# ScalarE takes copies, one table set for the residual norms, and softmax sums turned on TensorE

## The chip, the cores and the metric

The kernel runs on one core of a Trainium2 chip. The core has TensorE (PE, matrix products into PSUM), VectorE (DVE), ScalarE (ACT), GpSimd (POOL) and SyncE (SP), which here issues the DMAs. The engines run side by side and wait for each other through semaphores; each engine and each DMA-issuing queue works its own instructions in program order. The metric is the device time of one execution in microseconds (us), from the first instruction to the last, all data in float32. Every product of two matrices is made of three matmuls: both factors are split into a high and a low part, and high by high, low by high and high by low are summed (lines L165 to L167).

## The reference

A network of four layers on a sequence of 1024 tokens with 1024 features: a gated linear attention (GLA), a dilated sliding-window attention (SWA), a differential attention (DA) and a latent attention (MLA). Behind each stands a residual with a norm. The parts that the change touches:

```python
def layer_norm(x, g, b):                      # behind GLA and SWA
    mu = jnp.mean(x32, axis=-1, keepdims=True)
    xc = x32 - mu
    var = jnp.mean(xc * xc, axis=-1, keepdims=True)
    return (xc * lax.rsqrt(var + LN_EPS) * g + b)
...
def _rmsnorm(x, g):                           # ahead of DA and MLA, in both, and at the end
    return x * lax.rsqrt(jnp.mean(x * x, axis=-1, keepdims=True) + RMS_EPS_2) * g
...
def block(qb):                                # DA, 128 queries by 1024 keys, 8 heads
    sc = jnp.einsum('bqhcd,bkhcd->bhcqk', qb, k) * scale
    p = jax.nn.softmax(sc, axis=-1)
    p = p[:, :, 0] - lam * p[:, :, 1]
    return jnp.einsum('bhqk,bkhd->bqhd', p, v)
...
o = _rmsnorm(o, subln_g) * (1.0 - lambda_init)
o = o * jax.nn.silu(z)
return o @ w_out
...
q = _rmsnorm(q_a, q_a_norm_g) @ w_q_b         # MLA's low-rank products
kv = _rmsnorm(c_kv, kv_a_norm_g) @ w_kv_b
```

## The kernel before

All activations lie transposed, features on the 128 partitions and tokens along the row, so a norm's sum over features is a product with a matrix of ones on PE. The program runs GLA (to about 395 us of the span), a boundary (to 545), SWA (to 1215), a boundary (to 1346), DA (V products and modulation to 1460, its main loop to 1991, a drain to 2018), a boundary (to 2148), MLA (low-rank products to 2290, the rest to 2690) and the last boundary, which ends the program.

**A boundary** (`boundary`) takes the attention output `o` and the gate `z` from DRAM for each of 8 feature tiles and 2 halves of the tokens: `gated` computes Silu(z)*o, 16 calls in all, the result split into `oh` and `ol`. It multiplies by the output weights, adds the residual, squares (L706, sums in `acc`), sums on PE (`stat`, L717), and makes 1/sqrt as Exp(-0.5*Ln(mean+eps)) on ACT: `rstd`, L722 and L723. A layer norm ahead of a modulated norm calls `rstd` twice per half. Then come the scaled tiles `t` (L773, L774) and their halves `xh` (L775) and `xl`, on which the next stage's first products wait. Silu, Ln and Exp need tables on ACT; where the next function isn't in the set at hand, an ACT_TABLE_LOAD stands ahead of it, put there by the build.

**Fill** work is queued as units of small pieces (a product's feature tiles) in `Fill`, and given out between the steps of a stage by a budget. `u_t` makes 128x512 products, `u_v` 128x256 ones, both in PSUM tiles `mm` that turn over, so a tile that isn't copied out holds up a later product. The copies out: `u_gate` (L254, z to DRAM; half 0 on ACT, half 1 on DVE), SWA's V (L959) and DA's V (L1285, both alternately DVE and ACT), MLA's low-rank results `lraw` (L1485, DVE, followed by Square on ACT, L1487). `lownorm` norms these (L1506 Ln, L1507 Exp, L1510 scaling on DVE). `u_ada` computes modulation columns: DVE multiplies rows of a streamed weight by a scalar and adds up (`xb`, L575 to L577), PE sums the partitions with ones (L583).

**DA's main loop** has 64 iterations, 8 heads of 8 query blocks. Each makes scores of two softmaxes (`sc`, L1420), a maximum on DVE (L1424), Exp on ACT with the sum of a row in `d0` (`dsum`) and `den` (L1426), and one iteration later their combination on DVE (L1441 to L1443). Two iterations later P is transposed on PE (`attend`, L1240) and split on ACT and DVE into `PTh` and `PTl` (`PTl` at L150), and after each second block `pv` multiplies by V (L1365 to L1368) and writes `y` to DRAM as `d_o`. The norm of DA's output is put off: `norm` writes sums of squares to DRAM (`d_ms`), `combine` writes the softmax sums (`d_dn`, L1445), and `factors` reads both back as `vr` (L1251, L1252) in another layout, computes an inverse square root by four Newton steps on DVE (L1254 to L1265) and writes `d_rs`, which the boundary reads. It is called after the norm of head 6 for 14 half heads (tiles 128x56), once for (7,0) (128x4) and in the boundary for (7,1).

**The order** of PE in DA's loop is written out as in the code; the other engines and SP's queue are set by a scheduler that simulates the program. A DMA that has to wait holds all behind it on SP.

## Time and profile before

| what | us |
|---|---|
| median of 3 runs | 2798.11 (2795.3 to 2800.18) |
| the profiled execution's own time | 2794.63 |
| its span | 2792.9 |
| PE busy in it | 2660.9 (95%) |
| DVE busy | 1890.0 (68%) |
| ACT busy | 1349.2 (48%) |

The profile is of one execution. An engine's busy time is the sum of its instructions; a waiting engine shows idle time ahead of an instruction, with the engine, line and operation that released it. The granted clock of TensorE is given as a share of full speed, 2.4 GHz; half of it is 1.2 GHz. Times inside the profile are microseconds from the start of the span.

### The profile page before, as it was taken

The page shows a single profiled execution, that of the slowest core. Times are in us where ns is not written, and L with a number is a line of the kernel's source. Part 1 is how long each engine was busy: PE and PEld are TensorE (multiplying, and loading weights), DVE is VectorE, ACT ScalarE, POOL GpSimd, SP SyncE. Part 2 cuts the span into 40 slices and gives each one's busy share as a digit, 9 for nine tenths or more (in the row PEclk, how much of TensorE's full clock was granted, in tenths as well). Part 3 has the DMA queues.
Part 4 walks back from the last instruction along what each step waited for, and adds up shares of the span by engine and source line. Part 5 has one row for each costly group of instructions (what it writes and reads, how often), then busy time and mean ns, then how long its engine had stood idle before and what let it go on. Part 6 is the DMA issues. An engine that isn't in the chain of part 4 may idle for free.

```text
span 2792.9 us, 39308 instructions
## 1 busy us (share of the span) xinstructions
PE 2660.9 (95%) x14788; PEld 2234.5 (80%) x14788; DVE 1890.0 (68%) x3478; ACT 1349.2 (48%) x2492; POOL 314.6 (11%) x224
## 2 busy tenths in 40 slices
PE   8999999998999999988999999998799899999998
PEld 7889988887778878776897877786578688888878
DVE  7776547567666666667657788886576627777785
ACT  5444345426344434347515766765445415554563
POOL 0000000000000000000015656664000000000000
PEclk9999999999999999999999999999799999999999
DMA  5310155654111111154642432342275220100143
GB/s 206 107 43 32 49 180 182 210 176 144 50 42 50 46 47 53 50 185 145 228 165 74 63 67 61 66 55 62 90 266 170 68 70 23 33 27 29 39 172 110
DMA packets 163926, 274.70 MB, mean 98 GB/s; under 512 B 32948, under 2 KB 82388, under 8 KB 162072
## 3 DMA queue, kind: packets, MB, share of 16 engines
q1 hardware_dynamic: 163736, 272.19, 31.7%
q8 instruction: 116, 1.90, 0.3%
q14 instruction: 74, 0.61, 0.1%
HBM read 195.48 MB, written 66.17 MB: 94 GB/s over the span
## 4 chain that ended last, share of the span: by engine, by line
PE 67%; DVE 14%; DMA 7%; ACT 7%; issue 3%; SPq 1%; POOL 1%; ACTq 0%; DVEq 0%; POOLq 0%
PE mm L165 14%; PE mm L166 14%; PE mm L167 14%; PE pt L1240 3%; PE sc L1420 3%; PE sc L1657 2%; PE sc L1049 2%; PE lv L489 1%; PE pt L1153 1%; PE sc L166 1%; PE sc L165 1%; PE sc L167 1%; DVE den L1424 1%; PE mm L1623 1%; DVE wlo L150 1%
## 5 line engine op out<-in xcount | busy, mean ns | idle before, releaser
L165 PE MATMUL mm<-xh,whi 128*128 128x512 f32 x1456 | 613.3, 421 | 18.0 <-DVE t L911 6.0
L167 PE MATMUL mm<-xh,wlo 128*128 128x512 f32 x1456 | 574.0, 394 | 2.5 <-POOL wlo L150 1.6
L166 PE MATMUL mm<-xl,whi 128*128 128x512 f32 x1456 | 574.0, 394 | 1.7 <-DVE xl L150 1.7
L165 PEld LDWEIGHTS mm<-xh,whi 128*128 128x128 f32 x1456 | 277.6, 191 | 75.5 <-DVE t L911 7.3
L167 PEld LDWEIGHTS mm<-xh,wlo 128*128 128x128 f32 x1456 | 275.8, 189 | 64.4 <-POOL wlo L150 2.5
L166 PEld LDWEIGHTS mm<-xl,whi 128*128 128x128 f32 x1456 | 277.6, 191 | 52.9 <-DVE xl L150 4.0
L150 POOL TENSOR_TENSOR wlo<-wraw,whi 128x1024 fp32r<-128x1024 f32 x29 | 70.6, 2435 | 1334.9 <-ACT whi L192 1332.9
L165 PE MATMUL mm<-wvhi,xh 128*128 128x256 f32 x704 | 204.6, 291 | 4.8 <-DVE V L959 3.0
L192 ACT CAST whi<-wraw 128x1024 fp32r<-128x1024 f32 (+2 forms) x141 | 135.9, 964 | 138.3 <-PE mm L166 128.9
L167 PE MATMUL mm<-wvhi,xl 128*128 128x256 f32 x704 | 199.2, 283 | 0.1
L166 PE MATMUL mm<-wvlo,xh 128*128 128x256 f32 x704 | 198.6, 282 | 0.0
L1426 ACT ACTIVATE P<-sc,den 128x1024 f32<-128x1024 f32 x128 | 142.9, 1117 | 113.4 <-DVE den L1424 112.8
L1424 DVE TENSOR_REDUCE den<-sc 128x1 f32<-128x1024 f32 x128 | 153.5, 1212 | 3.5 <-PE sc L1420 3.5
L150 DVE TENSOR_TENSOR wlo<-wraw,whi 128x1024 fp32r<-128x1024 f32 (+2 forms) x113 | 123.5, 1093 | 43.8 <-ACT whi L192 40.7
L1043 ACT ACTIVATE P<-P,nm 128x128 f32<-128x128 f32 (+1 forms) x192 | 84.9, 443 | 124.5 <-DVE nm L1041 124.2
L165 PEld LDWEIGHTS mm<-wvhi,xh 128*128 128x128 f32 x704 | 134.0, 190 | 9.9 <-DVE V L959 3.2
L166 PEld LDWEIGHTS mm<-wvlo,xh 128*128 128x128 f32 x704 | 134.5, 191 | 1.3 <-issue 1.0
L167 PEld LDWEIGHTS mm<-wvhi,xl 128*128 128x128 f32 x704 | 133.9, 190 | 0.4 <-DVE xl L150 0.4
L165 PE MATMUL mm<-oh,xh 128*128 128x512 f32 (+1 forms) x336 | 126.1, 375 | 0.3 <-ACT oh L796 0.3
L166 PE MATMUL mm<-ol,xh 128*128 128x512 f32 (+1 forms) x336 | 124.2, 370 | 2.0 <-DVE ol L150 2.0
L167 PE MATMUL mm<-oh,xl 128*128 128x512 f32 (+1 forms) x336 | 123.7, 368 | 0.0
L1053 DVE CUSTOM_DVE_ANT_0 P<-sc,band 128x128 f32<-128x128 f32 (+1 forms) x192 | 59.6, 348 | 71.5 <-PE sc L1049 71.1
(355 smaller groups left out, 6124.5 us busy)
## 6 DMA issues: line engine op xcount, KB each, us to landing
xa<-in_ada_w SPq DMA_DIRECT2D x12, 2048.0 KB
d_z<-zt SPq DMA_DIRECT2D x64, 256.0 KB
oh<-d_z SPq DMA_DIRECT2D x64, 256.0 KB
ol<-d_o SPq DMA_DIRECT2D x64, 256.0 KB
d_r<-X SPq DMA_DIRECT2D x48, 256.0 KB
wraw<-in_swa_wq SPq DMA_DIRECT2D x24, 512.0 KB
res<-d_r SPq DMA_DIRECT2D x40, 256.0 KB
zt<-zt SPq DMA_DIRECT2D x160, 64.0 KB
```

Source lines behind the costliest of these rows:

```text
L150: eng.tensor_tensor(out, src, hi.bitcast(F32), op=OP.subtract)
L165: mm(ps, l[0], r[0], start=first, stop=False)
L166: mm(ps, l[0], r[1], start=False, stop=False)
L167: mm(ps, l[1], r[0], start=False, stop=last)
L192: nc.scalar.copy(hi, raw)
L1043: S.activation(p[:, off:off + w_], p[:, off:off + w_], AF.Exp, bias=nm[:, g, b:b + 1], scale=scale, accum_out=stat(h, g, 1, b))
L1049: T.matmul(sc[:, b % 2, :w_], q[:, b * 128:b * 128 + 128], k[:, k0:k0 + w_], start=True, stop=True)
L1053: V.tensor_tensor_reduce(p[:, off:off + w_], sc[:, b % 2, :w_], mk, 1.0, NEG, op0=OP.add, op1=OP.max, accum_out=stat(h, g, 0, b))
L1240: nc.tensor.transpose(pt[:, i, :], P[:, (4 * j + i) * 128:(4 * j + i) * 128 + 128], self.ident)
L1420: T.matmul(sc[c][:, s], QS[h][c][r, q0:q0 + 128], (KL[h] if k else KH[h][c])[r, s], start=first, stop=not first)
L1424: V.tensor_reduce(dn[:, 2 + c:3 + c], sc[c], AX, OP.max, negate=True)
L1426: S.activation(p, sc[c], AF.Exp, bias=dn[:, 2 + c:3 + c], accum_out=dn[:, 1:2] if c else d0)
```

## The change

Six edits, of which the fourth has two places.

1. `tables`: an explicit load of table set 6, which holds Ln and Exp, is put behind the 16th Silu of each boundary. The build's loads at L722, L723, L1506 and L1507 go: 11, 11, 3 and 3 loads; 4 new ones come.
2. Copies out of PSUM on ACT: all of SWA's V (12 move from DVE), all of DA's V (16), MLA's `lraw` (10), and half 1 of the gate in MLA's low-rank part (8).
3. The softmax sums are turned on PE: instead of a DMA that scatters `dsum` (128 partitions by 4 elements) into `d_dn` element by element, `pv` transposes it into an unused part of its PSUM bank, ACT copies the 4x128 result to `dr` and SP writes four rows of 512 bytes. There are 16 of these.
4. `factors` issues its reads where it did, and returns its arithmetic, `rest`, which the loop calls two iterations later. In DA's V products the modulation units `ada` stand further back among the V units; in MLA's low-rank part the last one stands behind two gate units.
5. One tile of ones serves both uses.
6. In GLA, in SWA's loop and in DA's, the gate keeps its engines (`act=False`).

```diff
+    def tables(self, n, behind):
+        nc = self.nc
+        with self.tc.issue_after(behind.ins):
+            return nc.scalar.add_instruction(mybir.InstLoadActFuncSet(
+                act_func_set_id=n, name=nc.get_next_instruction_name(), engine=mybir.EngineType.Activation))
...
-            (self.nc.vector.tensor_copy if hf else self.nc.scalar.copy)(z, ps)
+            (self.nc.scalar.copy if act or not hf else self.nc.vector.tensor_copy)(z, ps)
...
-            S.activation(g, z, AF.Silu)
+            silu = S.activation(g, z, AF.Silu)
+            if len(O) == 15:
+                self.tables(6, silu)
...
-                        (S.copy if st % 2 else V.tensor_copy)(Vt[g][:, st, :], ps)
+                        S.copy(Vt[g][:, st, :], ps)
...
+        def rest():
+            V.scalar_tensor_tensor(e, e, 128.0 * 1e-6, e, op0=OP.mult, op1=OP.mult)
+            V.tensor_tensor(t, t, e, op=OP.add)
...
+        return rest
...
-                    (S.copy if st % 2 else V.tensor_copy)(t, ps)
+                    S.copy(t, ps)
...
-                    pre.add(u_vs(0, range(4, 8)), u_vs(1, range(4, 5)), ada[0], u_vs(1, range(5, 8)), ada[1], u_vs(2, range(0, 4)), ada[2], u_vs(2, range(4, 8)), ada[3], u_vs(3, range(0, 4)), ada[4], u_vs(3, range(4, 8)), ada[5])
+                    pre.add(u_vs(0, range(4, 8)), u_vs(1, range(4, 8)), ada[0], u_vs(2, range(0, 3)), ada[1], u_vs(2, range(3, 6)), ada[2], u_vs(2, range(6, 8)), u_vs(3, range(0, 1)), ada[3], u_vs(3, range(1, 4)), ada[4], u_vs(3, range(4, 8)), ada[5])
...
-                o = self.mmp.tile([128, 256], F32, name="mm")
+                bank = self.mmp.tile([128, 512], F32, name="mm")
+                o, d = bank[:, :256], bank[0:4, 256:384]
...
+                if due:
+                    T.transpose(d, due[0][2], self.ident)
...
+                if due:
+                    g, hf, _ = due.pop()
+                    r = dp.tile([128, 128], F32, name="dr")
+                    S.copy(r[0:4], d)
+                    nc.sync.dma_start(self.dnd[g][:, half(hf)].rearrange("o (f p) -> (o f) p", p=128), r[0:4])
...
-                    self.factors(dp, FACT[h, qb4])
+                    return self.factors(dp, FACT[h, qb4])
...
+                if facts and facts[0][0] <= i:
+                    facts.pop()[1]()
...
-                            nc.sync.dma_start(self.dnd[h][:, half(t // 4)].rearrange("o (f p) -> (o p) f", p=128),
-                                              dsum[:, t - 3:t + 1])
+                            due.append((h, t // 4, dsum[:, t - 3:t + 1]))
...
-                        V.tensor_copy(raw[key, hf][:, c, :], ps)
+                        S.copy(raw[key, hf][:, c, :], ps)
...
-                pre.add(self.u_ada(p0, 1, 5, 1), *[self.u_gate(h, "mla_wz", p0) for h in range(3, 8)])
+                late = [self.u_gate(h, "mla_wz", p0) for h in range(3, 8)]
+                pre.add(*late[:2], self.u_ada(p0, 1, 5, 1), *late[2:])
```

Lines below L254 move down by 6 to 24 in the new file (L722 is L728, L775 is L781, L1251 is L1260, L1254 is L1265, L1255 is L1266, L1485 is L1508). What stands where, at the three places that matter most, first ACT in the boundary to DA, where the norm of the second half is made between the modulated tiles of the first (`t` and the halves `xh_70`), before:

```order
L774 ACTIVATE t<-t,mods,gsc 128x512
L722 ACT_TABLE_LOAD
L722 ACTIVATE rs<-stat,cv 128x512
L775 CAST xh_70<-t 128x512
L204 CAST wvhi<-wvraw 128x512
L723 ACT_TABLE_LOAD
L723 ACTIVATE rs<-rs 128x512
L204 CAST wvhi<-wvraw 128x512
```

and now:

```order
L780 ACTIVATE t<-t,mods,gsc 128x512
L728 ACTIVATE rs<-stat,cv 128x512
L781 CAST xh_70<-t 128x512
L204 CAST wvhi<-wvraw 128x512
L729 ACTIVATE rs<-rs 128x512
L204 CAST wvhi<-wvraw 128x512
```

Both loads are gone from between the tiles, and the rest stands as it did. Next SP's queue at the end of DA's loop, iterations 58 to 62, where the sums for the factors go out and come back, before:

```order
L255 DMA d_z<-zt 128x512
L1381 DMA d_ms<-sq 1x256
L179 DMA wraw<-in_w_out 128x1024
L1251 DMA vr<-d_ms 128x4
L1445 DMA d_dn<-dsum 128x4x1
L1371 DMA d_o<-y 128x256
L255 DMA d_z<-zt 128x512
L179 DMA wraw<-in_w_out 128x1024
L1381 DMA d_ms<-sq 1x256
```

and now:

```order
L1387 DMA d_o<-y 128x256
L1392 DMA d_dn<-dr 4x128
L1261 DMA vr<-d_dn 128x4
L255 DMA d_z<-zt 128x512
L1402 DMA d_ms<-sq 1x256
L179 DMA wraw<-in_w_out 128x1024
L1260 DMA vr<-d_ms 128x4
L1387 DMA d_o<-y 128x256
L255 DMA d_z<-zt 128x512
L179 DMA wraw<-in_w_out 128x1024
L1402 DMA d_ms<-sq 1x256
```

The write of `d_dn` is a row of four descriptors behind a `d_o`, with its read next to it, and none stands behind the read of `d_ms`; that read is still behind a weight load. Last DVE in the same iterations, the first operation of the arithmetic on 14 half heads, before:

```order
L1443 SCALAR_TENSOR_TENSOR P<-P,den 128x1024
L1254 SCALAR_TENSOR_TENSOR vr<-vr 128x56
L150 TENSOR_TENSOR PTl<-pt,PTh 128x4x128
L1424 TENSOR_REDUCE den<-sc 128x1
L150 TENSOR_TENSOR PTl<-pt,PTh 128x4x128
```

and now, three iterations later:

```order
L150 TENSOR_TENSOR PTl<-pt,PTh 128x4x128
L1447 TENSOR_REDUCE den<-sc 128x1
L1265 SCALAR_TENSOR_TENSOR vr<-vr 128x56
L1465 RECIPROCAL den<-den 128x1
L1466 SCALAR_TENSOR_TENSOR den<-den,nlam,dsum 128x1
L254 COPY zt<-mm 128x512
L1467 SCALAR_TENSOR_TENSOR P<-P,den 128x1024
L150 TENSOR_TENSOR PTl<-pt,PTh 128x4x128
L1447 TENSOR_REDUCE den<-sc 128x1
L150 TENSOR_TENSOR PTl<-pt,PTh 128x4x128
L1447 TENSOR_REDUCE den<-sc 128x1
L1266 TENSOR_TENSOR vr<-vr 128x56
```

The first operation has moved from between iterations 55 and 56 to between 58 and 59; the second (L1255, now L1266) stays between 59 and 60.

## Rows read from the trace of the kernel before

**Rows 1.** The page: busy time of each engine, its share of the span, and its instructions.

```profile
PE 2660.9 (95%) x14788; PEld 2234.5 (80%) x14788; DVE 1890.0 (68%) x3478; ACT 1349.2 (48%) x2492; POOL 314.6 (11%) x224
```

**Rows 2.** The page: the chain of work that ended last, shares of the span by engine.

```profile
PE 67%; DVE 14%; DMA 7%; ACT 7%; issue 3%; SPq 1%; POOL 1%; ACTq 0%; DVEq 0%; POOLq 0%
```

**Rows 3.** The table of stretches; the columns are the stretch, its length, then busy microseconds (and instructions) of PE, PE's weight loads, DVE, ACT and POOL, the granted TensorE clock as a share of full speed, the DMA engines' share, and GB/s. From the top: the boundary to DA, DA's V products, 26 iterations of DA's main loop, the loop's last stretch, its drain up to the boundary to MLA, and two pieces of MLA's low-rank products.

```profile
1300.00:1346.00 46.00, 38.84 (x167) 28.66 (x168) 34.74 (x49) 40.42 (x60) 4.81 (x2) 0.93 0.50 164
1346.00:1395.00 49.00, 45.34 (x355) 43.15 (x356) 30.61 (x51) 19.09 (x33) 0.00 (x0) 1.00 0.60 211
1500.00:1900.00 400.00, 398.91 (x2253) 319.34 (x2252) 326.34 (x387) 272.91 (x510) 255.51 (x181) 1.00 0.36 62
1917.00:1966.00 49.00, 38.92 (x197) 29.72 (x195) 26.89 (x44) 22.37 (x44) 12.89 (x8) 0.90 0.19 57
1966.00:2019.00 53.00, 37.99 (x169) 29.13 (x169) 30.95 (x65) 25.58 (x47) 2.19 (x3) 0.73 0.26 74
2140.00:2224.00 84.00, 77.52 (x334) 62.14 (x334) 48.87 (x71) 45.07 (x62) 0.00 (x0) 1.00 0.28 90
2224.00:2240.00 16.00, 11.78 (x38) 8.49 (x37) 8.77 (x13) 1.66 (x2) 0.00 (x0) 0.79 0.42 134
```

**Rows 4.** PE's waits over the whole span: who waited for whom, microseconds in total, times, the longest.

```profile
PE pt L1240 <- DVE PTl L150: 16.2, 4, 6.1
...
PE mm L165 <- DVE V L959: 3.0, 1, 3.0
```

**Rows 5.** ACT's timeline in the boundary to DA; the columns are start, duration, engine, line, operation, and in brackets the idle time before it and its releaser.

```profile
1321.20 1.28 ACT L722 ACT_TABLE_LOAD   x1
...
1323.08 0.61 ACT L775 CAST xh<-t 128x512 fp32r<-128x512 f32 x1
```

**Rows 6.** PE's timeline in the same boundary and in DA's V products behind it.

```profile
1323.74 0.80 PE L165 MATMUL mm<-xh,whi 128*128 128x512 f32 x1 [1.62 <-ACT xh L775]
...
1381.44 1.10 PE L583 MATMUL mm<-xb,ones 128*128 128x512 f32 x2 [2.94 <-DVE xb L577]
```

**Rows 7.** DVE's timeline in DA's V products, the copy ahead of the second of these waits.

```profile
1372.79 0.42 DVE L1285 COPY vs<-mm 128x256 f32<-128x256 f32 x1 [5.33 <-PE mm L167]
```

**Rows 8.** PE's timeline over DA's last iterations and the drain, the rows that waited.

```profile
1903.42 0.50 PE L165 MATMUL mm<-xh,whi 128*128 128x512 f32 x1 [2.51 <-ACT y L1370]
...
1928.97 1.11 PE L1240 MATMUL pt<-ident,P 128*128 128x128 f32 x4 [5.44 <-DVE PTl L150]
...
1965.95 0.66 PE L1240 MATMUL pt<-ident,P 128*128 128x128 f32 x4 [3.91 <-DVE PTl L150]
1967.89 1.08 PE L1240 MATMUL pt<-ident,P 128*128 128x128 f32 x4 [1.29 <-DVE vr L1264]
...
1999.47 1.97 PE L1240 MATMUL pt<-ident,P 128*128 128x128 f32 x8 [6.11 <-DVE PTl L150]
```

**Rows 9.** DVE's timeline there: the first steps of the factors' arithmetic.

```profile
1928.10 0.22 DVE L1254 SCALAR_TENSOR_TENSOR vr<-vr 128x56 f32<-128x56 f32 x1 [7.03 <-DMA vr<-d_dn]
...
1962.55 0.22 DVE L1255 TENSOR_TENSOR vr<-vr 128x56 f32<-128x56 f32 x1 [9.08 <-DMA vr<-d_ms]
...
1998.66 0.16 DVE L1255 TENSOR_TENSOR vr<-vr 128x4 f32<-128x4 f32 x1 [6.66 <-DMA vr<-d_ms]
```

**Rows 10.** The chain of work that ended last, in order of time, its DMA steps there: start, duration, what.

```profile
1879.20 10.11 DMA d_dn<-dsum
...
1915.26 10.25 DMA d_dn<-dsum
1925.52 2.47 DMA vr<-d_dn
...
1952.72 9.70 DMA vr<-d_ms
```

**Rows 11.** MLA's low-rank products: DVE's timeline, two rows.

```profile
2172.71 1.41 DVE L1510 SCALAR_TENSOR_TENSOR lraw<-lraw,vecs,lrs 128x512 f32<-128x512 f32 x2 [3.34 <-ACT lrs L1507]
...
2175.53 1.29 DVE L1485 COPY lraw<-mm 128x512 f32<-128x512 f32 x2
```

**Rows 12.** PE's timeline there, the waits of the same products and of the modulation's second sum.

```profile
2176.28 0.50 PE L165 MATMUL mm<-xh,whi 128*128 128x512 f32 x1 [2.43 <-DVE lraw L1485]
...
2219.53 0.47 PE L165 MATMUL mm<-xh,whi 128*128 128x512 f32 x1 [1.70 <-DVE zt L254]
...
2230.67 2.08 PE L583 MATMUL mm<-xb,ones 128*128 128x512 f32 x2 [4.22 <-DVE xb L577]
```

**Rows 13.** The end of the program: ACT's and DVE's timeline.

```profile
2783.04 1.28 ACT L722 ACT_TABLE_LOAD   x1
...
2784.83 1.28 ACT L723 ACT_TABLE_LOAD   x1
...
2786.57 2.77 DVE L765 TENSOR_TENSOR X<-X,rs 128x256 f32<-128x256 f32 x8 [3.16 <-ACT rs L723]
```

**Rows 14.** Copies out of PSUM by line and engine: count, shortest, median and longest in ns, first and last start.

```profile
L254 ACT COPY zt<-mm x32: 561/586/591, 121.6 to 2283.7; 128x512 f32<-128x512 f32 x32
L254 DVE COPY zt<-mm x32: 673/691/692, 128.8 to 2289.1; 128x512 f32<-128x512 f32 x32
```

**Rows 15.** ACT's casts of streamed weights: the DMAs that its idle time ahead of them waited for (microseconds in total, times).

```profile
  DMA wvraw<-in_swa_wv: 9.3, 4
...
  DMA wvraw<-in_da_wv: 4.6, 5
```

More of the change, by code (lines that the diff above doesn't have):

```diff
@@ L248, in u_v, with u_gate @@
         return u
-    def u_gate(self, h, src, pool, halves=(0, 1), w=None):
+    def u_gate(self, h, src, pool, halves=(0, 1), w=None, act=True):
         def evac(hf, s, ps):
             z = self.wp.tile([128, 512], F32, name="zt", bufs=2)
-            (self.nc.vector.tensor_copy if hf else self.nc.scalar.copy)(z, ps)
+            (self.nc.scalar.copy if act or not hf else self.nc.vector.tensor_copy)(z, ps)
             self.nc.sync.dma_start(self.zd[h][hf], z)
@@ L274, in build @@
             self.ident = cp.tile([128, 128], F32, name="ident")
-            self.ones = cp.tile([128, 128], F32, name="ones")
             self.ones_r = cp.tile([128, 128], F32R, name="ones_r")
+            self.ones = self.ones_r.bitcast(F32)
             self.cv = cp.tile([128, 4], F32, name="cv")
@@ L283, in build @@
             nc.vector.memset(self.ones, 1.0)
-            nc.vector.memset(self.ones_r.bitcast(F32), 1.0)
             for i, v in enumerate((1.0, 1e-5, 1e-6, 0.0)):
@@ L345, in u_g @@
             def u_g(h, halves=(0, 1)):
-                return self.u_gate(h, "gla_wg", gp, halves)
+                return self.u_gate(h, "gla_wg", gp, halves, act=False)
             nc.sync.dma_start(self.vecs, A["vecs"])
@@ L836, in boundary @@
                 if normed and hf == 0 and kt == 7:
-                    self.factors(bo, [(7, 1)])
+                    self.factors(bo, [(7, 1)])()
                 gated(hf, kt)
@@ L1201, in after @@
                         fill.add(u_kk(1, 0))
-                    fill.add(self.u_gate(h, "swa_wg", ap, (0, 1) if h > 2 else (1,)))
+                    fill.add(self.u_gate(h, "swa_wg", ap, (0, 1) if h > 2 else (1,), act=False))
             for g in range(3):
@@ L1252, in factors @@
             nc.sync.dma_start(e[:, 4 * n:4 * n + 4], flat(self.dnd[g], hf))
-        V.scalar_tensor_tensor(e, e, 128.0 * 1e-6, e, op0=OP.mult, op1=OP.mult)
-        V.tensor_tensor(t, t, e, op=OP.add)
-        V.tensor_scalar(t, t, 1.0 / 128.0, None, op0=OP.mult)
-        yi = y.bitcast(I32)
-        V.tensor_scalar(yi, t.bitcast(I32), 1, None, op0=OP.logical_shift_right)
-        V.tensor_scalar(yi, yi, -1.0, float(0x5f3759df), op0=OP.mult, op1=OP.add)
-        V.tensor_scalar(t, t, -0.5, None, op0=OP.mult)
-        for _ in range(4):
-            V.tensor_tensor(e, y, y, op=OP.mult)
-            V.tensor_tensor(e, e, t, op=OP.mult)
-            V.scalar_tensor_tensor(y, e, 1.5, y, op0=OP.add, op1=OP.mult)
-        for n, (g, hf) in enumerate(hs):
-            nc.sync.dma_start(flat(self.rsd[g], hf), y[:, 4 * n:4 * n + 4])
+        def rest():
+            V.scalar_tensor_tensor(e, e, 128.0 * 1e-6, e, op0=OP.mult, op1=OP.mult)
+            V.tensor_tensor(t, t, e, op=OP.add)
+            V.tensor_scalar(t, t, 1.0 / 128.0, None, op0=OP.mult)
+            yi = y.bitcast(I32)
+            V.tensor_scalar(yi, t.bitcast(I32), 1, None, op0=OP.logical_shift_right)
+            V.tensor_scalar(yi, yi, -1.0, float(0x5f3759df), op0=OP.mult, op1=OP.add)
+            V.tensor_scalar(t, t, -0.5, None, op0=OP.mult)
+            for _ in range(4):
+                V.tensor_tensor(e, y, y, op=OP.mult)
+                V.tensor_tensor(e, e, t, op=OP.mult)
+                V.scalar_tensor_tensor(y, e, 1.5, y, op0=OP.add, op1=OP.mult)
+            for n, (g, hf) in enumerate(hs):
+                nc.sync.dma_start(flat(self.rsd[g], hf), y[:, 4 * n:4 * n + 4])
+        return rest
     def da(self, before):
@@ L1349, in da @@
             fill = Fill()
-            zs = [self.u_gate(h, "da_wz", dp, (hf,)) for hf, h in [(1, h) for h in range(3)] +
+            zs = [self.u_gate(h, "da_wz", dp, (hf,), act=False) for hf, h in [(1, h) for h in range(3)] +
                   [(hf, h) for h in range(3, 8) for hf in range(2)]]
@@ L1382, in norm @@
                 if (h, qb4) in FACT:
-                    self.factors(dp, FACT[h, qb4])
+                    return self.factors(dp, FACT[h, qb4])
             FACT = {(6, 3): [(h, hf) for h in range(7) for hf in range(2)], (7, 1): [(7, 0)]}
-            nrm, comb = None, []
+            nrm, comb, due, facts = None, [], [], []
             for i in range(64 + 2):
@@ L1435, in da @@
                     if nrm and j % 2:
-                        norm(*nrm)
+                        if f := norm(*nrm):
+                            facts.append((i + 2, f))
                         nrm = None
```

## The prediction, made before the changed kernel ran

> **What bounds the kernel now.** First the busy times: PE works 95% of the span [rows 1], so 132 us of the span are idle PE, and no edit that only relieves another engine can win more than that, plus what a low clock costs. The chain of waits agrees: 67% PE, 14% DVE, 7% DMA, 7% ACT [rows 2]. Then the table of stretches, to see where the idle time lies [rows 3]. DA's main loop has none to give: 398.9 of 400 us busy at full clock. The boundary to DA has 46.0 - 38.84 = 7.2 us at a clock of 0.93, the V products behind it 3.7 us, DA's last iterations 10.1 us at 0.90, the drain 15.0 us at 0.73, MLA's low-rank products 6.5 us and, in their last 16 us, 4.2 us at 0.79. Last I went by PE's list of waits: the longest entry is the transposes of DA that wait for `PTl`, 16.2 us in four waits [rows 4], all in DA's end [rows 8].
>
> **The change, part by part.** Everything is summed against the profiled execution, 2794.63 us, which is 3.5 us under the median of 2798.11; I subtract the sum from the median.
>
> *DA's end, -20.* The big gaps go back to read-backs. DVE stops at L1254 for 7.0 us and at L1255 for 9.1 and 6.7 us [rows 9], each time for a read-back into `vr`; the splits to `PTl` stand behind it in DVE's order, and PE runs dry for 5.44, 3.91 + 1.29 and 6.11 us [rows 8]. Behind the reads stands the scattered write of `d_dn`: it lands after 10.1 to 10.25 us for 2 KB, and its read, which may only start then, 2.47 us later [rows 10]. Until it lands that read also holds SP, and with it the transfers queued behind it, the rotary embedding's `zt` among them; ACT works in order, a step on `zt` stands ahead of a copy of `y`, and PE's gap of 2.51 us is that copy [rows 8], 14 us behind the landing at 1889, so I put it to the scatter too. And the read of `d_ms` that DVE needs at 1962 takes 9.70 us with such a write issued right behind it and a weight load ahead. The new write is four long rows. The new place of L1265 is three iterations on, at 64 iterations in some 530 us about 24 us, so the 5.44 goes, whatever the write takes. The second operation keeps its place; its read is still behind 512 KB of weights, but no scatter is on the rings. I take 4 to 5 us for it, between the 2.47 of a lone read and the 9.70: then DVE still stops for some 3 us, which PE's work in hand covers for the most part. Waits that go: 2.5 + 5.4 + 3.9 + 1.3 + 5 of the last 6.1 = 18.1. The granted clock dropped to 1.2 GHz after these gaps. The loss in the last iterations is at most 49 x 0.10 = 4.9 us and in the drain 53 x 0.27 = 14.3 us, part of it over idle time; of the whole I count 6. I take 4 off, for the read of `d_ms` and for L1266, which at (7,0) now stands ahead of the combination of the last iteration. -20, between -8 (only the first two gaps go) and -27.
>
> *Boundary to DA and the V products, -9.* Eight loads of 1.28 us are in ACT's order through this boundary's norms, one replaces them. ACT is busy 40.4 of 46 us there [rows 3], so it is the engine that sets the tiles' pace: a load at 1321.20 stands between two of them, and PE waits 1.62 us for the next `xh` [rows 5, 6]. I take half of the 7.2 us idle, 3.6, and 2.8 of the 3.2 (46 x 0.07) that the clock cost. In the V products DVE idles 5.33 us in a copy L1285 that waits for PE [rows 7], then is late with `xb`, and PE waits 2.94 us [rows 6]; with the copies on ACT and `ada` further back this wait goes: 2.6. Sum 9; ends -4 (the two named waits alone) and -12.
>
> *MLA's low-rank products, -11.* A copy L1485 on DVE stands behind L1510, which waits 3.34 us for ACT's Exp, itself behind two loads [rows 11]; PE waits 2.43 us for that copy. It waits 1.70 us for a gate copy and 4.22 us for the last modulation unit [rows 12], after which the clock loses 16 x 0.21 = 3.4 us. The copies move to ACT, whose queue loses six loads; the unit moves behind two gate units, 2 x 16 feature tiles of three matmuls, each 77.52 us / 334 = 0.23 us [rows 3], some 22 us of cover. 8.35 + 3.4 = 11.7; I take 11, since ACT then has two jobs on the same result, copy and Square. Ends -6 (unit and gate copy alone) and -13.5.
>
> *End of the program, -1.8.* The second load, 1.28 us, lies bare on the path to the last scaling. Of the first, 0.7 us lie beside PE's sum; 0.57 is bare [rows 13]. Ends -1.5 and -2.
>
> A rule of the Trainium skill bears on this term. In the trace the second load begins 1.79 us after the first one, which is 1.28 plus the Ln between them: no time is lost behind a load [rows 13]. The page "ScalarE: Activation LUTs" (What ACT_TABLE_LOAD costs) gives 1283 ns and a drain of about 1380 ns, 2.66 us for each switch. The load's own length agrees; the drain isn't seen. An estimate by that page makes this term about -4.5, and the whole 2757 in place of 2760.
>
> *DA's main loop, +2.5.* Here PE is the bound, so 16 added transposes count in full. Four transposes of P took 1.11 us at half clock [rows 8], so one is 0.14 us at full: 2.2, with a little for `mm`, which is held for a copy more. Ends +1.6 and +4. ACT's 16 copies are short, beside 273 of 400 us busy [rows 3].
>
> *SWA's V copies, 0.* One wait of 3.0 us is for such a copy on DVE [rows 4]. On ACT it is not bound by DVE's work any more, but it stands behind casts of streamed weights, which wait for DMAs [rows 15]. Ends -3.5 and +2.
>
> *Nothing:* one memset; the loads in the other boundaries, beside their products, and those of GLA, which stay.
>
> Sum: -20 - 9 - 11 - 1.8 + 2.5 + 0 = -39.3, rounded down to -38 for what I can't place; 2798.1 - 38 = 2760.
>
> **The rivals.** *The read of `d_ms` sets DA's end.* Its 9.70 us may be the weight load's doing, not the scatter's. For it: the load is issued 0.4 us ahead of it and still is. Against it: 512 KB at the 200 GB/s of a busy stretch [rows 3] are 2.6 us. Then only 2.5 + 5.4 of the waits go, with some 2 to 4 of the clock: this part gives -10 and the whole is 2798 - 28 = 2770.
>
> *The gaps move.* In the boundary ACT or DVE may be the true bound, as 40.4 of 46 us busy says [rows 3]; a wait for `xh` becomes a wait for `xl`, and in MLA ACT takes 18 more copies of 0.59 us [rows 14], 10.5 us, so that PE waits for them instead. Then the boundary gives 3, MLA 3, DA's end 15: about 2798 - 20 = 2778.
>
> A rule of the Trainium skill speaks the same way: TensorEngine Tiling (Array Packing) (PSUM Bottleneck) says "Use both ScalarE and VectorE for PSUM evacuation", and the change gives all of three lines to one. What the trace can say is that the copy is shorter on ACT, 586 against 691 ns [rows 14], so the rule hangs on the queue, not on the copy.
>
> *Slower.* ACT takes its work in order. If each of the 28 copies of V stands behind a cast that waits for its weights, 13.9 us in 9 waits or 1.5 us in the mean, at most 2.3 [rows 15], PSUM fills up and PE waits with it: 28 x 1.5 = 43 us, or 65 at 2.3. From 38 / 28 = 1.4 us each on the kernel is slower; the time would be 2803 to 2825. Against it: there are more PSUM tiles than one, and the casts run ahead of their products, in 50 us of the V products only 19.1 us of ACT are busy [rows 3].
>
> *It doesn't do what it says.* The explicit load could be followed by loads of the build all the same; the order of the new kernel shows none behind it, so I give this no chance of its own.
>
> **How the numbers follow.** The forecast has 0.62, the read that stays 0.18, the gaps that move 0.15, slower 0.05. All favourable ends together are -3.5 - 12 + 1.6 - 27 - 13.5 - 2 = -56, 2742; all unfavourable ones +2 - 4 + 4 - 8 - 6 - 1.5 = -13.5, 2784.6. The range, 2742 to 2784, holds the forecast and the first two rivals, and leaves out the third. A measurement of this kernel can tell about 0.2%, 5.6 us, from no change. Faster by more than that: 0.62 + 0.18 + 0.12 = 0.92, with 0.03 of the moving gaps to within it, and 0.02 of the last; slower 0.03.
>
> **What would show it.** Right: 40 loads in all on ACT where 64 were; PE's waits for `PTl` below 4 us in all; no write of `d_dn` above 4 us; the stretch from 1966 at a clock above 0.85; no wait of 4 us for `xb` in MLA; the last scaling some 1.8 us earlier behind its sum; 16 transposes of 0.14 us. Wrong: a wait at L1266 of more than 6 us (first rival); PE's waits for ACT copies, L1485's successor above all, of more than 6 us (second); waits of PE for V behind casts (third).

## The result, and the profile after

Median 2754.76 us of 4 runs (2752.13 to 2758.27), against 2799.14 us for the kernel before on the same chip (4 runs, 2795.3 to 2800.56): ratio 0.9844, 95% interval [0.9827, 0.9861]. The profiled execution took 2754.68 us with a span of 2752.9, 40.0 less than the span before; by the medians it is 44.4, since the profiled execution of the kernel before lay 4.5 under its median. The forecast was 2760.

The page of the changed kernel, busy times and the chain of work that ended last, against [rows 1, 2]:

```profile
PE 2651.4 (96%) x14804; PEld 2232.2 (81%) x14804; DVE 1873.2 (68%) x3431; ACT 1337.4 (49%) x2530; POOL 312.7 (11%) x224
...
PE 70%; DVE 14%; DMA 7%; ACT 5%; issue 3%; SPq 1%; POOL 0%; DVEq 0%; ACTq 0%; POOLq 0%
```

Idle PE fell from 132 to 101.5 us; busy PE fell by 9.5 us in spite of 16 matmuls more, since less of it ran at the low clock. The table of stretches of the changed kernel, cut at the same places of the program as [rows 3], but for the middle of the loop, which is the same time window in both, and with the same columns:

```profile
1295.00:1340.00 45.00, 40.13 (x173) 29.77 (x172) 36.01 (x50) 35.47 (x57) 4.81 (x2) 0.92 0.55 172
1340.00:1390.00 50.00, 48.05 (x377) 46.89 (x377) 22.61 (x35) 21.05 (x40) 0.00 (x0) 0.97 0.60 208
1500.00:1900.00 400.00, 396.25 (x2248) 316.70 (x2247) 329.43 (x386) 272.46 (x524) 253.34 (x180) 1.00 0.22 61
1913.00:1947.00 34.00, 33.67 (x188) 26.08 (x187) 26.81 (x43) 22.65 (x45) 12.96 (x8) 1.00 0.26 82
1947.00:1992.00 45.00, 33.97 (x183) 26.75 (x181) 30.94 (x64) 25.21 (x49) 2.91 (x4) 0.92 0.27 77
2112.00:2187.00 75.00, 73.86 (x323) 60.00 (x321) 38.32 (x56) 43.23 (x69) 0.00 (x0) 1.00 0.29 95
2187.00:2202.00 15.00, 15.00 (x68) 12.43 (x67) 10.81 (x15) 3.65 (x5) 0.00 (x0) 1.00 0.44 145
```

DA's end is 34 + 45 us where it was 49 + 53, with 11.4 us of idle PE in place of 25.1, and the clock is 1.00 and 0.92 where it was 0.90 and 0.73. MLA's low-rank products run at full clock to their end. The first two stretches, the boundary to DA and its V products, hardly changed.

Where each part of the 40 us lies is read best from landmarks, the same instruction found in both timelines:

| landmark | before | after | lead | gained since the last |
|---|---|---|---|---|
| PE's first product in the boundary to DA | 1211.82 | 1210.24 | 1.6 | 1.6 |
| PE's sum for the norm of the second half there | 1345.88 | 1339.80 | 6.1 | 4.5 |
| DVE's first combination in DA's loop | 1486.41 | 1482.47 | 3.9 | -2.1 |
| the 53rd combination | 1890.15 | 1890.35 | -0.2 | -4.1 |
| ACT's first Square in MLA's low-rank products | 2142.32 | 2114.75 | 27.6 | 27.8 |
| PE's first scores in MLA | 2307.12 | 2268.99 | 38.1 | 10.6 |
| end of the span | 2792.9 | 2752.9 | 40.0 | 1.9 |

A gain of a microsecond or two ahead of the boundary to DA means nothing: of the kernels below, those with the same code up to there reach SWA's first scores between 631.2 and 636.7 us. The later landmarks spread too, since each comes from a single profile of its kernel. In the kernels below with the same code for a stretch as the changed kernel, this one included, the boundary to DA up to PE's sum for the second half takes 128.2 to 129.7 us (ten kernels), the V products from there to the first scores in DA 131.1 to 133.4 (six), and MLA's low-rank products from the first Square to the first scores 154.2 to 154.3 (eight). In the nine kernels with all softmax sums turned, DA's loop from the first combination to the 53rd takes 406.1 to 409.4 us and its end from there to MLA's first Square 220.8 to 227.2. Two kernels have the boundary and the V products of the kernel before: 134.1 and 132.3 us, and 129.7 and 130.7. So a difference of a microsecond tells something in MLA's low-rank products and little elsewhere.

### The profile page after: what moved, and what is told of

Read it like the earlier page. It is cut to its first block, busy times and chain, and to the rows that moved or that the text cites. A ratio compares the mean times of both kernels' runs of the same rounds, so it can differ in the third digit from the quotient of the medians.

```text
span 2752.9 us, 39334 instructions
## 1 busy us (share of the span) xinstructions
PE 2651.4 (96%) x14804; PEld 2232.2 (81%) x14804; DVE 1873.2 (68%) x3431; ACT 1337.4 (49%) x2530; POOL 312.7 (11%) x224
## 4 chain that ended last, share of the span: by engine, by line
PE 70%; DVE 14%; DMA 7%; ACT 5%; issue 3%; SPq 1%; POOL 0%; DVEq 0%; ACTq 0%; POOLq 0%
PE mm L165 15%; PE mm L166 15%; PE mm L167 15%; PE pt L1248 3%; PE sc L1443 3%; PE sc L1681 2%; PE sc L1057 2%; PE lv L495 1%; DVE den L1447 1%; DVE P L1467 1%; PE pt L1161 1%; DVE wlo L150 1%; PE mm L1647 1%; PE sc L166 1%; ACT P L1449 1%
## 5 line engine op out<-in xcount | busy, mean ns | idle before, releaser
L192 ACT CAST whi<-wraw 128x1024 fp32r<-128x1024 f32 (+2 forms) x141 | 136.0, 964 | 135.9 <-PE mm L166 126.9
```

What stands on the lines that cost most here:

```text
L192: nc.scalar.copy(hi, raw)
```

## The experiments

Each run was timed with the kernel before on the same chip; the ratio is to that, with its 95% interval. "Landmarks" are those of the table, against the changed kernel unless another is named.

### The scattered softmax sums

**Sums scattered again, arithmetic still late.**

```diff
-                            due.append((h, t // 4, dsum[:, t - 3:t + 1]))
+                            nc.sync.dma_start(self.dnd[h][:, half(t // 4)].rearrange("o (f p) -> (o p) f", p=128),
+                                              dsum[:, t - 3:t + 1])
```

> The changed kernel with the softmax sums scattered from dsum to DRAM as before, so without the 16 transposes, their copies and their row writes; the arithmetic of the factors stays two iterations late. Theory (the scattered write holds SP and the read of d_ms): the read of d_ms takes 9 us again in place of 3.2, DVE stops for it for some 8 us, the wait for the copy of y near iteration 53 is back: 12 us more in DA's last iterations and drain, 4 us less in the main loop without the transposes; together about 2763. Rival (calling the arithmetic late is what removed the waits): nothing back at the end, the loop 4 us shorter, about 2751.

Measured: 2777.02 us, 0.9922 [0.9905, 0.9938]. By the landmarks the loop is 3.6 us shorter and its end 24.5 us longer; I had expected 12. DVE's timeline in that end:

```profile
1926.07 0.22 DVE L1265 SCALAR_TENSOR_TENSOR vr<-vr 128x56 f32<-128x56 f32 x1 [6.91 <-DMA vr<-d_dn]
...
1957.43 0.22 DVE L1266 TENSOR_TENSOR vr<-vr 128x56 f32<-128x56 f32 x1 [5.08 <-DMA vr<-d_ms]
...
1991.64 0.17 DVE L1266 TENSOR_TENSOR vr<-vr 128x4 f32<-128x4 f32 x1 [5.75 <-DMA vr<-d_ms]
```

All three stops of [rows 9] are back, with the arithmetic called two iterations late. The chain of waits of this run, its DMA steps from there on, shows that the scatter delays its neighbours too: the write of 1 KB that is `d_ms` is in it with 7.11 us.

```profile
1913.33 9.98 DMA d_dn<-dsum
1923.33 2.64 DMA vr<-d_dn
...
1951.61 5.70 DMA vr<-d_ms
1982.82 7.11 DMA d_ms<-sq
```

**Arithmetic called at once, sums turned.**

```diff
-                            facts.append((i + 2, f))
+                            f()
```

> The changed kernel with the arithmetic of the factors called at once, where the reads are issued. Theory (the scatter was the cause, and the read of d_dn is long back): within 2 us of the changed kernel, 2753 to 2757. Rival (the late call is needed): DVE stops some 5 us at the first or second operation, PE runs dry for 4 to 5 us and the clock falls, about 2761.

Measured: 2755.78 us, 0.9844 [0.9830, 0.9859]; from the first combination to MLA's first Square it differs from the changed kernel by 0.2 us. The late call does nothing: the first step stands 43.4 us behind the 53rd combination in both kernels, so the scheduler puts it there by itself. Whether a step that stood earlier would wait isn't shown by this run.

**The kernel before with turned sums alone** (and one tile of ones, for the space).

```diff
+                if due:
+                    T.transpose(d, due[0][2], self.ident)
...
+                    S.copy(r[0:4], d)
+                    nc.sync.dma_start(self.dnd[g][:, half(hf)].rearrange("o (f p) -> (o f) p", p=128), r[0:4])
```

> The kernel before with the softmax sums turned on PE and written as rows, and one tile of ones for both uses, which frees the space for that; nothing else. Theory (the scatter is the whole cause of the waits at DA's end): 24 us less there, 4 us more in the loop, 2798 - 20 = 2778. Rival (the late arithmetic is needed too): a stop of DVE at the first operation near iteration 56, some 10 us less gained, 2788.

Measured: 2774.96 us, 0.9911 [0.9893, 0.9929]. From the 53rd combination to MLA's first Square it gains 24.9 us on the kernel before; the loop loses 3.2. DVE's timeline at the two steps on 14 half heads:

```profile
1937.92 0.21 DVE L1253 SCALAR_TENSOR_TENSOR vr<-vr 128x56 f32<-128x56 f32 x1
...
1948.01 0.22 DVE L1254 TENSOR_TENSOR vr<-vr 128x56 f32<-128x56 f32 x1 [2.84 <-DMA vr<-d_ms]
```

The scheduler has moved the first step late by itself here, and the second waits as short as in the changed kernel. Taken out of the changed kernel or put alone into the old one, the turned sums are worth 24.5 and 24.9 us at DA's end: they are nearly the whole of the 27.8 us won there, and the rest lies inside the spread of that stretch.

**Sums of heads 0 to 5 scattered, those of heads 6 and 7 turned.**

```diff
-                            due.append((h, t // 4, dsum[:, t - 3:t + 1]))
+                            if h < 6:
+                                nc.sync.dma_start(self.dnd[h][:, half(t // 4)].rearrange("o (f p) -> (o p) f", p=128),
+                                                  dsum[:, t - 3:t + 1])
+                            else:
+                                due.append((h, t // 4, dsum[:, t - 3:t + 1]))
```

> The changed kernel with the softmax sums of heads 0 to 5 scattered by DMA as before, and only those of heads 6 and 7 turned on PE. Theory (a scatter hurts only where its read-back waits for it; in the loop the 12 turned ones cost PE 0.3 us each): the loop from its first to its 53rd combination 3 us shorter than in the changed kernel, its end unchanged, about 2751. Rival (the loop's 4 us come from something else in it): 2755.

Measured: 2748.57 us, 0.9828 [0.9811, 0.9845]. From the first combination to the 53rd it is 4.2 us shorter than the changed kernel, as long as the kernel before to 0.1 us and under all nine kernels with all sums turned, and the end is no longer. It is the fastest of all by its median; its interval overlaps that of the changed kernel, so that it beats it is shown by the landmarks rather than by the times.

### The table loads

**The changed kernel without its explicit loads.**

```diff
-            if len(O) == 15:
-                self.tables(6, silu)
```

> The changed kernel without its four explicit loads, so that the build puts the 28 loads back. Theory (the loads cost the boundary to DA 5 us, MLA's low-rank products 2 to 3, the end 1.8): 9 us slower than the changed kernel, about 2764, with the sum on PE for the second half's norm in the boundary to DA 5 us later than there. Rival (the loads were hidden beside products everywhere but at the end, and the copies and the order of the units brought the rest): 2 us slower, about 2757.

Measured: 2771.81 us, 0.9900 [0.9885, 0.9914]; the span is 13.0 us longer, the median 17.1, as the profiled execution was the quickest of its four. The boundary to DA is 3.1 us longer to the sum of the second half, MLA's low-rank products 7.4, the end 1.8; another 2.0 lie ahead of that boundary, where they can't be told from the spread. PE's waits in MLA's low-rank products of this run:

```profile
PE mm L165 <- ACT lraw L1506: 3.3, 2, 3.1
PE mm L167 <- DVE wlo L150: 2.3, 1, 2.3
```

With the copy on ACT, a load ahead of Exp stands ahead of the copy itself, and the loads cost 7.4 us here against 5.3 in the kernel before (the next run). The theory's side is right and its size too small: the loads were not hidden, and they cost more than the 9 us I gave them.

**The kernel before with the four explicit loads alone.**

```diff
-            S.activation(g, z, AF.Silu)
+            silu = S.activation(g, z, AF.Silu)
+            if len(O) == 15:
+                self.tables(6, silu)
```

> The kernel before with the four explicit loads alone, 40 loads in place of 64. Theory (the loads were worth 13 us, as leaving them out of the changed kernel showed): about 2785, 2 us in the boundary to SWA, 4 to 5 in that to DA, 4 or more in MLA's low-rank products, 1.8 at the end. Rival (what they give in MLA hangs on the copies and units that stand elsewhere in the changed kernel): 2789 to 2791.

Measured: 2783.56 us, 0.9942 [0.9925, 0.9959]; the span is 12.6 us shorter than before, the median 15.6. The boundary to DA gains 5.5, the V products lose 1.6 (to PE's first scores in DA), MLA's low-rank products gain 5.3, the end 1.8. PE's waits in MLA's low-rank products of this run, the copies still on DVE:

```profile
PE mm L590 <- DVE xb L584: 4.2, 1, 4.2
PE mm L165 <- DVE xb L593: 1.0, 1, 1.0
PE mm L165 <- DVE lraw L1494: 0.3, 1, 0.3
```

The wait for `lraw`, 2.8 us in all before, is 0.3, and that for the gate copy isn't in the list: the loads made both. The modulation's 4.2 us stay.

DA's loop and end need a word, since nothing in them was changed: the loop up to the 53rd combination is 7.9 us longer than in the kernel before, the stretch behind it 6.3 shorter. One of PE's stops for `PTl` lies ahead of the landmark here, with a read of `d_ms` of 7.83 us in the chain ahead of it:

```profile
1886.40 1.12 PE L1249 MATMUL pt<-ident,P 128*128 128x128 f32 x4 [4.83 <-DVE PTl L150]
```

So where the scatter's stops fall varies, and loop and end are safer together: 653.2 to 657.5 us in the three kernels that scatter all sums, 629.4 to 634.2 in the nine that turn them all, 625.9 and 627.5 in the two that turn four, the one with mixed sums and the last one below. By that measure the turned sums are worth 20.9 us in the changed kernel and 21.7 in the kernel before.

### The copies and the modulation's places

**MLA's low-rank copies on DVE.**

```diff
-                        S.copy(raw[key, hf][:, c, :], ps)
+                        V.tensor_copy(raw[key, hf][:, c, :], ps)
```

> The changed kernel with MLA's ten low-rank copies on DVE as before. Theory (the copy itself was late because it stood on DVE behind a scaling that waited for Exp): the wait of 2.4 us comes back smaller, 1 to 2 us, since the loads ahead of Exp are gone: 2756 to 2757. Rival (the loads were all of it): no difference, 2755; second rival (DVE at its limit there): 4 us or more.

Measured: 2754.93 us, 0.9839 [0.9825, 0.9854]; the low-rank products are 1.4 us shorter by the landmarks, which is clear of the 0.1 us by which kernels with the same code differ there; the time is the same. With the loads gone the move of these ten copies to ACT gains nothing and costs 1.4 us.

**MLA's last modulation unit ahead of all late gates.**

```diff
-                pre.add(*late[:2], self.u_ada(p0, 1, 5, 1), *late[2:])
+                pre.add(self.u_ada(p0, 1, 5, 1), *late)
```

> The changed kernel with the last modulation unit of MLA's low-rank part in its old place, ahead of all late gates. Theory (cover of some 22 us for DVE's sums): the wait of PE for xb of about 4 us and the low clock behind it are back, MLA's scores start 4 to 7 us later, about 2760. Rival (DVE was late only because its scalings waited for the table loads, which are gone): within 1 us, 2755.

Measured: 2762.74 us, 0.9875 [0.9860, 0.9890]; MLA's scores start 4.8 us later, counted from its first Square. The wait is back:

```profile
PE mm L589 <- DVE xb L583: 3.7, 1, 3.7
```

**DA's V copies on both engines.**

```diff
-                    S.copy(t, ps)
+                    (S.copy if st % 2 else V.tensor_copy)(t, ps)
```

> The changed kernel with the 32 copies of DA's V products alternately on DVE and ACT as before, the modulation units in their new places. Theory (all copies on in-order ACT cost the V products some 3 us: ACT waits 3.2 us for a store of vs to free its buffer and PE runs dry for 1.95 us behind it): the start of DA's loop 2 to 3 us earlier than in the changed kernel, about 2752. Rival (the copies on DVE are what made the modulation's sums late before): 3 us later, about 2758.

Measured: 2753.66 us, 0.9845 [0.9829, 0.9862]. From PE's sum for the second half to its first scores in DA it takes 133.1 us, the changed kernel 131.1, the kernel before 129.7. That is inside the spread of 131.1 to 133.4, so neither the 2 to 3 us earlier nor the 3 us later is seen, and PE still waits 2.7 us for `vs`.

**The modulation of DA's V products in its old places.**

```diff
-                    pre.add(u_vs(0, range(4, 8)), u_vs(1, range(4, 8)), ada[0], u_vs(2, range(0, 3)), ada[1], ...
+                    pre.add(u_vs(0, range(4, 8)), u_vs(1, range(4, 5)), ada[0], u_vs(1, range(5, 8)), ada[1], ...
```

> The changed kernel with the modulation units of DA's V products in their old places, the copies all on ACT. Theory (the new places only move the wait for xb, which is 2.7 us in the changed kernel too): within 2 us of the changed kernel at the start of DA's loop. Rival (they gained what I forecast, 2.6 us): 2.6 us later or more, about 2758.

Measured: 2754.19 us, 0.9845 [0.9830, 0.9860]; the same stretch takes 129.0 us, 2.1 under the least of the six kernels with the new places. These gained nothing, and may have cost 2 us or more; in this run PE doesn't wait for `vs` at all.

**Six buffers for `vs`.**

```diff
-                    t = vp.tile([128, 256], F32, name="vs", bufs=3)
+                    t = vp.tile([128, 256], F32, name="vs", bufs=6)
```

> The changed kernel with six buffers in place of three for vs, the tile that DA's V products are copied to ahead of their store. Theory (ACT's queue is held by a buffer whose store has not landed): no wait of ACT for d_v, PE's wait of 1.95 us and the low clock behind it gone, the start of DA's loop 2 to 3.5 us earlier, about 2752. Rival (the copies come late for ACT's other work): no change, 2755.

Measured: 2753.14 us, 0.9840 [0.9825, 0.9854]; the same stretch takes 126.9 us, 4.2 under the least of the six. The wait of PE for `vs` is 0.3 us in place of 1.9.

**Mixed sums, six buffers and old places together.**

```diff
+                            if h < 6:
...
+                    t = vp.tile([128, 256], F32, name="vs", bufs=6)
...
+                    pre.add(u_vs(0, range(4, 8)), u_vs(1, range(4, 5)), ada[0], u_vs(1, range(5, 8)), ada[1], ...
```

> As the run with sums scattered for heads 0 to 5, and with six buffers for vs and the modulation units of DA's V products in their old places. Theory (the three gains lie in different stretches): 3 us from the loop, 2 to 4 from the V products: 2747 to 2750. Rival (buffers and places take away the same wait, and the stretch is bound by DVE's sums): as the run with mixed sums alone, within 1 us.

Measured: 2749.18 us, 0.9824 [0.9810, 0.9837], the same as mixed sums alone, and the stretch takes 131.9 us in both. By the time the rival holds, but the run doesn't settle whether the gains add. With the old places the first modulation sum comes early enough for PE to wait for it, and it starts when the transfer of the modulation's weights has landed. DVE's and PE's timeline there in the run with the old places alone:

```profile
1365.46 0.49 DVE L581 TENSOR_SCALAR xb<-xa,sc 128x512 f32<-128x512 f32 x1 [8.31 <-DMA xa<-in_ada_w]
...
1372.69 2.05 PE L589 MATMUL mm<-xb,ones_r 128*128 128x512 f32 x2 [2.79 <-DVE xb L583]
```

and in this run:

```profile
1369.02 0.49 DVE L581 TENSOR_SCALAR xb<-xa,sc 128x512 f32<-128x512 f32 x1 [10.43 <-DMA xa<-in_ada_w]
...
1376.12 2.05 PE L589 MATMUL mm<-xb,ones_r 128*128 128x512 f32 x2 [4.79 <-DVE xb L583]
```

SP issues the transfer 18.5 us behind PE's sum for the second half in both, but DVE gets to start 27.6 us behind that sum in the one and 29.8 in the other, and PE waits 2.0 us longer. Among the six kernels with the changed kernel's code in this stretch that start lies between 27.7 and 29.1. In the kernel before it came at 27.6 too: DVE idled 5.33 us in a copy [rows 7], and then 0.3 us for the same transfer.

## Why the prediction was right, and where it was wrong

The time, the sign and the range held: 2754.8 against 2760, 44 us gained where 38 were forecast. Of the terms, two were near and three were off. That their sum came so close, 39.3 us forecast ahead of rounding and 40.0 us of span measured, is in part luck: 7.8 us too little at DA's end stand against 6.6 too much in the boundary and the V products and 1.6 in the loop.

**DA's end: the cause was right, the size too small.** Forecast -20, measured -27.8. The scatter was the cause: 24.5 us by taking it back, 24.9 by taking it out alone, 20.9 and 21.7 with the loop counted in; no other edit shows a part in it. DVE's timeline of the changed kernel, against [rows 9]:

```profile
1933.72 0.20 DVE L1265 SCALAR_TENSOR_TENSOR vr<-vr 128x56 f32<-128x56 f32 x1
...
1943.55 0.22 DVE L1266 TENSOR_TENSOR vr<-vr 128x56 f32<-128x56 f32 x1 [2.54 <-DMA vr<-d_ms]
...
1970.84 0.16 DVE L1265 SCALAR_TENSOR_TENSOR vr<-vr 128x4 f32<-128x4 f32 x1 [1.86 <-DMA vr<-d_dn]
...
1972.48 0.34 DVE L1266 TENSOR_TENSOR vr<-vr 128x4 f32<-128x4 f32 x1 [1.16 <-DMA vr<-d_ms]
```

and the read that I had put at 4 to 5 us, in its chain of waits, against [rows 10]:

```profile
1940.26 3.17 DMA vr<-d_ms
```

It took 3.17 us with the weight load still ahead of it, so the first rival, that the load set those 9.70 us, is refuted. Two sizes were off. Of the 4 us that I took off for the waits left over only some 2 were spent: the last two stretches were to lose 18.1 - 2.5 - 4 = 11.6 us of idle time and lost 13.7. PE waits 2.9 us for `PTl` in the whole span where it waited 16.2 [rows 4], 1.5 of them in DA's end; the line is among those further below. And the clock gave back more than the 6 us counted: in the last two stretches the length fell by 102 - 79 = 23 us, of which 25.1 - 11.4 = 13.7 is idle time, so 9.3 is shorter busy time for much the same products (371 instructions against 366), which ran at 2.4 GHz where they had run at 1.2 after the gaps; another 4 us were won ahead of them, where I had 2.5. The late call of the arithmetic, on which the prediction leaned for the wait at L1254, was not needed.

**DA's loop: sign right, size too small.** Forecast +2.5, measured +4.1. The price of a transpose itself holds. PE's timeline around one of them:

```profile
1547.18 0.39 PE L167 MATMUL mm<-xh,wlo 128*128 128x512 f32 x1
1547.41 0.27 PE L1379 MATMUL mm<-ident,dsum 128*4 128x128 f32 x1
1547.44 0.36 PE L1381 MATMUL mm<-PTh,vh 128*128 128x256 f32 x1
1547.64 0.28 PE L1382 MATMUL mm<-PTh,vl 128*128 128x256 f32 x1
```

The second product behind it (L1382) starts 0.46 us after the last one of the fill, where without a transpose that is 0.34: 0.12 us each, 2 us for 16. The rest is idle time, 400 - 396.25 = 3.75 us of the loop's middle where it was 1.09 [rows 3]; it falls to 1.69 in the mixed version, which scatters 12 of the sums, so most of it is theirs. Which of the copy, the bank held longer or the scheduler's other order makes it was not told apart.

**Boundary to DA and V products: wrong.** Forecast -9, measured -4.5 + 2.1 = -2.4. The boundary gave 4.5 of the 6.4 that I had put there, and the loads account for it: 3.1 us come back with them, 5.5 go with them alone. The wait of 1.62 us that I named is gone. But I had overlooked a wait for the tile ahead of it, and that one stayed. PE's timeline before:

```profile
1320.52 0.49 PE L165 MATMUL mm<-xh,whi 128*128 128x512 f32 x1 [1.77 <-ACT xh L775]
```

and PE's and ACT's now, against [rows 5, 6]:

```profile
1316.39 0.80 PE L165 MATMUL mm<-xh,whi 128*128 128x512 f32 x1 [1.85 <-ACT xh L781]
...
1315.20 0.62 ACT L204 CAST wvhi<-wvraw 128x512 fp32r<-128x512 f32 x1 [0.23 <-DMA wvraw<-in_da_wv]
1315.72 0.61 ACT L781 CAST xh<-t 128x512 fp32r<-128x512 f32 x1
...
1316.96 0.67 ACT L728 ACTIVATE rs<-stat,cv 128x512 f32<-128x512 f32 x1
1317.53 0.60 ACT L781 CAST xh<-t 128x512 fp32r<-128x512 f32 x1
```

That `xh` is made ahead of the Ln, behind casts of streamed weights that wait for their DMAs. And the 2.8 us that I counted for the clock did not come: it is 0.92 in this stretch where it was 0.93.

In the V products the step that failed is "with the copies on ACT and `ada` further back this wait goes". The named wait, ahead of the first modulation sum, went, but the copies had no part in it: with all copies on ACT and the old places it was 2.79 us. I took an idle DVE in a copy as the cause of a late `xb`; behind it stood a transfer that let DVE start as late, after 9.0 us of idle time in place of 5.3. DVE's timeline of the changed kernel:

```profile
1368.15 0.49 DVE L581 TENSOR_SCALAR xb<-xa,sc 128x512 f32<-128x512 f32 x1 [9.02 <-DMA xa<-in_ada_w]
...
1385.10 0.69 DVE L592 TENSOR_TENSOR xb<-mm,ident 128x512 f32<-128x512 f32 x1 [8.14 <-PE mm L589]
...
1388.32 0.49 DVE L581 TENSOR_SCALAR xb<-xa,sc 128x512 f32<-128x512 f32 x1
```

and PE's:

```profile
1384.04 1.02 PE L589 MATMUL mm<-xb,ones_r 128*128 128x512 f32 x2
...
1396.35 1.10 PE L589 MATMUL mm<-xb,ones_r 128*128 128x512 f32 x2 [2.66 <-DVE xb L583]
```

The new places cured the first wait and made the second. `xb` is ready at 1375.2, PE takes it at 1384.0, and there is one buffer of it, so DVE stands idle for 8.14 us and begins the second sum at 1388.3; for that one PE waits. PE's waits of the changed kernel over the whole span, against [rows 4]:

```profile
PE pt L1248 <- DVE PTl L150: 2.9, 3, 1.5
PE mm L589 <- DVE xb L583: 2.7, 1, 2.7
...
PE mm L165 <- ACT xh L781: 2.0, 2, 1.9
...
PE mm L165 <- ACT vs L1297: 1.9, 1, 1.9
```

A wait for `vs` is new. ACT's timeline says why that one came:

```profile
1373.39 0.71 ACT L1297 COPY vs<-mm 128x256 f32<-128x256 f32 x2 [3.22 <-DMA d_v<-vs]
```

The copy waits for a buffer whose store hasn't landed, and holds PE's PSUM. That is a small piece of the rival that ends slower, an in-order ACT held by a DMA, but by a store and not by the weights. The wait isn't there with the old places, stays with the copies on both engines, and is nearly gone with more buffers, so it comes from V units that stand closer together on three buffers rather than from the engine. (The 2.3 us that this rival took as the longest wait of a cast is the mean of four [rows 15]; the longest of them in the kernel before is 3.99 us.) How much the buffers and the old places give together is open.

**MLA's low-rank products: size right, one cause wrong.** Forecast -11, measured -10.6. I gave the copies' waits to the engine that copies. They came from the loads: 0.3 us of wait with the loads alone gone and the copies still on DVE, and a gain of 1.4 us rather than a loss with the copies put back. The modulation unit's place is worth 4.8 us, as the 4.22 us and the clock behind it had said, if less than both. Loads alone, place and copies are 5.3 + 4.8 - 1.4 = 8.7 of the 10.6; the rest was not told apart, and the gate's copies, which moved too, were not run by themselves.

**The end: right.** Forecast -1.8, measured -1.9. ACT's and DVE's timeline at the end of the changed kernel, against [rows 13]:

```profile
2745.62 0.47 ACT L728 ACTIVATE rs<-stat,cv 128x256 f32<-128x256 f32 x1 [0.79 <-PE stat L723]
2746.13 0.42 ACT L729 ACTIVATE rs<-rs 128x256 f32<-128x256 f32 x1
2746.58 2.77 DVE L771 TENSOR_TENSOR X<-X,rs 128x256 f32<-128x256 f32 x8 [1.36 <-ACT rs L729]
```

DVE waits 1.36 us for the factor where it waited 3.16: 1.8 less, one load bare and the bare part of the other. A drain behind each load would have made this some 4.5 us (an estimate by the Trainium skill, ScalarE: Activation LUTs, What ACT_TABLE_LOAD costs); the measurement speaks against it in this place.

**The second rival**, gaps that move, held for one stretch of three, DA's V products, where the wait for `xb` moved to the next sum, and not for the others. SWA's V copies were forecast at nothing, and nothing is to be seen.

## What to carry to other kernels

A wait named in a profile tells what came last, not what comes next: ahead of counting its removal, look for what else the waiting instruction needs, above all a transfer that lands at about the time when the work in front of it ends, and for what in turn waits for it, here the next sum in the same buffer. In this kernel transfers of single elements cost most where something reads them back at once, and the transfers beside them took longer, so the turn on TensorE paid at the read-back and not elsewhere: turning 4 of the 16 sums had all of the gain, and the loop paid nothing that could be seen. A difference of two microseconds between single profiles needs the spread of unchanged code beside it. Where a gap of some microseconds on PE goes, the time won is the gap and the half speed behind it, so price both.

## What the runs showed of the hardware that was not expected

A write of 2 KB in elements of 4 bytes took 9.5 to 10.25 us, and a read of 2 KB next to it 5.7 to 10.6 us (three kernels) where it took 3.2 to 3.5 in the same place without (four); a write of 1 KB beside one was in a chain of waits with 7.1 us. With rows of 512 bytes the write and its read-back didn't reach the chain of the changed kernel. The Trainium skill, DMA: Bandwidth & Descriptors (Specifications), says that transfers under 512 bytes aren't at full rate and become read-modify-write; the trace agrees that they are slow, and can't show what the DMA engines did.

At the end of the program an ACT_TABLE_LOAD cost its own 1.28 us and nothing more that could be seen. 24 of them fewer were worth 12.6 and 13.0 us of span, 15.6 and 17.1 by the medians: 0.5 to 0.7 us each, so a part of their time lay beside other work.
